# Two more column groups by seven products for eight: the third of the second eighth and the gate's first 512 columns

## The chip, the cores and the metric

The kernel runs on one core of a Trainium2 chip. TensorE (PE) multiplies; its weight loads (PEld) are shown apart. ScalarE (ACT) and VectorE (DVE) copy, round, add and apply functions, GpSimd (POOL) does a little arithmetic and issues some transfers, SyncE (SP) issues the weight transfers. The metric is the device time of one execution in microseconds; less is better. The time before is 2023.53 us, the median of 3 runs (2023.32 to 2023.73).

## The reference

Two layers over 256 positions of width 2048, batch 1, all in float32:

```python
h = rms_norm(x, norm1_g[l])
z = h @ w_in[l]
q, k, v, gu, gv = jnp.split(z, splits, axis=-1)        # 1024 columns each
attn = dilated_attention(rotary(q), rotary(k), v)      # 8 heads of 128
gm = chunked_gmlp(gelu(gu), gelu(gv), ln_g, ln_b, w_spatial, b_spatial)
x = x + concatenate([attn, gm]) @ w_out[l]
h2 = rms_norm(x, norm2_g[l])
x = x + square(relu(h2 @ w_up[l])) @ w_down[l]         # width 8192 between
```

and one last `rms_norm`. `chunked_gmlp` normalises its second argument (the columns `gv`, here "the gate") per group of 128, mixes it over positions with a masked 128x128 matrix per group, and multiplies by `gelu(gu)`.

## The kernel before

**Precision.** TensorE multiplies in a rounded form of float32 (`F32R`). Each factor is therefore split into a part hi, which ACT writes as a rounded copy, and a rest lo, which DVE writes as value minus hi. A product is the sum of three: hi by hi, hi by lo, lo by hi. So each block of weights of 128x1024 numbers (512 KB, one load of SP) costs ACT one copy (L168) and DVE one subtraction (L178) before TensorE can use it. The activations lie split in `hs` (the normalised input, L287 and L291), in `half` tiles (L646 and L649) and in `shared`.

**Three forms of product.** `transposed` (L376) keeps weights in the array and streams 256 positions: a step is 4 chunks of 128 rows by 256 columns, 24 matmuls of 256 columns. `natural` (L454) keeps activations in the array and streams 512 columns of weights: a step is 12 matmuls of 512. `fast` (L414) multiplies a block of 1024 rows by 512 columns as a 2 by 2 block matrix with seven products for eight (Winograd's form of Strassen's algorithm). It has two steps (p = 0, 1), called quick steps here, of 42 matmuls of 256 columns each: seven products of 2 chunks by 3 matmuls. Product by product, these use the weights' `top` block, `bottom` twice, `upper` twice and `lower` twice, where `upper` and `lower` are sums of blocks: four DVE additions (L219 to L224) on the raw weights. A quick step has two loads, but four blocks with a hi and a lo. It also needs sums of the left factor's blocks (four DVE additions, L803 to L806, then four times hi and lo). Its seven results lie in seven half banks of PSUM, and are added up later (`combine`, L815).

**Order.** The work is a list of steps written out by hand and traced once (L1007 to L1028). Every engine runs its instructions in the order in which this loop emits them. At step n it emits hi up to five loads ahead (`high_to`), what is due (`run_due`), lo up to four loads ahead (`low_to`), the loads of raw weights, then the step's matmuls, then what follows them (`after`, hooks), then at most 1.2 of cost from `queue` (`run_queue`). `later(delay, cost, fn)` and `soon(delay, fn)` count their delay in loads; a quick step counts as four (its four blocks). There are 6 hi and 6 lo buffers (L54 to L56), and 7 raw ones. A `mark` is a step without matmuls of its own; a `hook` runs behind the step with a given number.

**A layer.** `natural` over v (16 steps); `transposed` over k0, q0, k1, q1, k2, q2, k3, q3 (4 steps each, 32 in all, called q/k steps 0 to 31 here); `natural` over the gate (16 steps); `transposed` over gu (16) and over `w_out` (32). After each k or q follows its rotary (`after_qk`, L572: two ACT copies, three DVE operations); two loads after each q the scores of its two heads (`scores`, L587), before which the values of the previous two are multiplied (`values`); one load later the normalisation (`normalise`, L610), three loads later the transposes (`turn`). Behind each gate half come its gelu, statistics (`stats`, L672) and normalisation (`layer_norm`, L683, on POOL).

Then the MLP in eighths of 1024 hidden columns: stage e multiplies the e-th eighth of `w_up` (16 steps) and, one eighth behind, the rows of `w_down` of the eighth e - 1. Of the 2048 columns of `w_down`, the first 2 or 3 groups of 512 are done by quick steps, which are set before the steps that `ORDER` and `USUAL` (L63 to L66) name, one pair per group. The third group's partial results are added up in DRAM by POOL's transfers (`put`, L870). PSUM has 8 banks: 4 accumulators `acc`, of which the MLP's steps use two in turn, and 4 `aux`.

Of the kernel before, what the change touches and what calls it, by code (L numbers as in the profile page):

```python
# [61 lines left out]

ORDER = {1: ((7, 10), (13, 14)), 6: ((12, 15), (2, 3), (7, 8)), 7: ((7, 10), (2, 3)), 8: ()}  # L63
FINAL = (7, 7, 6)
# [3 lines left out]
HALVES = 5  # L68
BEHIND, BETWEEN = 2, 1
D_SCORES, D_NORM, D_TURN, D_VALUES = 2, 1, 3, 2  # L70

# [20 lines left out]
def trunk(ctx: ExitStack, tc: tile.TileContext, layout, xT, consts, gains, w, b_sp, w_sp, out):  # L92
# [8 lines left out]
    pacc = ctx.enter_context(tc.tile_pool(name="pacc", bufs=1, space=bass.MemoryType.PSUM))  # L101
    paux = ctx.enter_context(tc.tile_pool(name="paux", bufs=4, space=bass.MemoryType.PSUM))

# [31 lines left out]
    def acc_bank(i=None, of=4):  # L135
# [3 lines left out]
        return pacc.tile([P, 512], F32, name=f"acc{i}", tag=f"acc{i}")  # L139

    def aux_bank():
        return paux.tile([P, 512], F32, name="aux", tag="aux")

# [269 lines left out]

    def fast(name, l, row0, col0, tiles, slots, fresh, last, done):  # L414

# [5 lines left out]
        for p in range(2):  # L421
# [3 lines left out]
            def mm(p=p, top=top, bottom=bottom, upper=upper, lower=lower):  # L425
                if p == 0:
                    o.extend(slots())
                half = tiles[0][0]
                sums_ready()
                extra = sum_parts[0]  # L430
                left, right = slice(0, 256), slice(256, 512)
# [43 lines left out]
    def mark(fn):  # L475

        steps.append((None, fn, None))

    def from_hs(k):
# [38 lines left out]
    def layer(l, n1, n2, n3, last):  # L518
# [27 lines left out]
        if l:  # L546
            mark(start)
        mix_a, mix_g = [None], [None]
        qk = {}
# [37 lines left out]
        def scores(j, q, k):  # L587

            if turned:
                values(*turned.pop())  # L590
            s1, s0 = aux_bank(), aux_bank()
            for h in range(2):
                pe.matmul(s1[:, h * S:(h + 1) * S], lhsT=q[:, h, P:S], rhs=k[:, h, :], start=(h == 0), stop=True,  # L593
                          skip_group_check=True)
            for h in range(2):
                pe.matmul(s0[:, h * P:(h + 1) * P], lhsT=q[:, h, 0:P], rhs=k[:, h, 0:P], start=(h == 0), stop=True,  # L596
                          skip_group_check=True)
# [59 lines left out]
        def after_gv(c, ps):  # L657
            z, u = t32("gz", [2, 512], tag="tmpB"), t32("gu", [2, 512], tag="tmpA")
            for tt in range(2):
                act.activation(z[:, tt, :], ps[tt], AF.Copy, scale=n1.half[:, tt:tt + 1])  # L660

            def then(u, z):
# [4 lines left out]
                vec.scalar_tensor_tensor(par["y"][:, :, c:c + 512], u, 1.0, z, op0=OP.add, op1=OP.mult)  # L667
                later(1, 1.5, lambda: stats(c // P))

            gelu(z, u, then)  # L670

        def stats(g0):  # L672
# [8 lines left out]
            later(0, 1.0, lambda: layer_norm(g0))  # L681

        def layer_norm(g0):  # L683
            y, mv = par["y"], par["mv"]
            r = t32("lr", [2, 4])
            rsqrt(nc.gpsimd, r, mv[:, :, g0:g0 + 4, 1], 1.0, LN_EPS, [2, 4])
            for g in range(4):
                for tt in range(2):
                    yg = y[:, tt, (g0 + g) * P:(g0 + g + 1) * P]
                    nc.gpsimd.tensor_scalar(yg, yg, mv[:, tt, g0 + g, 0:1], r[:, tt, g:g + 1],  # L690
                                            op0=OP.subtract, op1=OP.mult)
            par["normed"] += 4
# [47 lines left out]
        hook(base + d + 6, rope)  # L740
        hook(base + d + 8, shift)
        for j in range(4):
            transposed("w_in", l, 0, KC, AW + j * 256, 256, from_hs, lambda c, ps, j=j: after_qk("k", j, ps))
            transposed("w_in", l, 0, KC, j * 256, 256, from_hs, lambda c, ps, j=j: after_qk("q", j, ps))
        natural("w_in", l, 4 * AW, AW, after_gv)
        transposed("w_in", l, 0, KC, 3 * AW, AW, from_hs, after_gu)
# [34 lines left out]
        def after_up(e):  # L781
            def f(c, ps):
# [17 lines left out]
        def sums():  # L800

            a11, a12, a21, a22 = (inner[:, 4 * k:4 * k + 4, t * P:(t + 1) * P] for t in range(2) for k in range(2))
            vec.tensor_tensor(a22, a21, a22, op=OP.add)  # L803
            vec.tensor_tensor(a21, a11, a21, op=OP.subtract)
            vec.tensor_tensor(a11, a22, a11, op=OP.subtract)
            vec.tensor_tensor(a12, a12, a11, op=OP.subtract)  # L806

# [4 lines left out]
            for k in range(0, 8, 2):  # L812
                later(0, 0.6, lambda k=k: parts(k))

# [33 lines left out]

        def halves(bank):
            return [bank[:, 0:256], bank[:, 256:512]]  # L850

        held = []
# [60 lines left out]
        for e in range(9):  # L913
# [3 lines left out]
            if e < 8:  # L917
                up = collect(transposed, "w_up", l, 0, KC, e * 1024, 1024, from_hs, after_up(e), of=2)
            if e:
                w = 512 * len(ORDER.get(e, USUAL))  # L920
                hidden = [hid[e - 1]]
                down = collect(transposed, "w_down", l, (e - 1) * 1024, 8, w, D - w, from_tiles(hidden, NH),
                               lambda c, ps, e=e, w=w: after_down(e, (c + w) // P, ps),
                               apart=last and e == 8, of=2 if e < 8 else 4,
                               cols=None if e < 8 else [c * P for c in LAST])
                for g, at in enumerate(ORDER.get(e, USUAL)):
                    banks = []
                    quick += zip(at, collect(fast, "w_down", l, (e - 1) * 1024, 512 * g, hidden,
                                             (lambda g=g, banks=banks: slots_other(g, banks)) if g else slots_first,
# [146 lines left out]
```

## Time and profile before

| | |
|---|---|
| median of 3 runs | 2023.53 us |
| the profiled execution, its time | 2023.7 us |
| its span in the profile | 2021.9 us |
| mean granted clock of TensorE | 0.997 |
| v, layer 0 | 7 to 51.6 us |
| q/k, layer 0 | 51.6 to 149.5 us |
| gate, layer 0 | 149.5 to 198.0 us |
| stage e = 1 (second eighth), layer 0 | 376.8 to 461.2 us |
| stage e = 3, layer 0 | 550 to 633 us |

The page gives each engine's busy time and share of the span, the chain of work that ended last, and groups of instructions with counts and mean durations. The trace behind it answers for windows of time, and lists instructions in order of time with the idle time before them and what ended it. Instructions of DVE and ACT overlap a little at their ends, so what counts in a sequence is the distance from start to start. A matmul's shown duration is longer than its slot, for the same reason.

### The profile page before, as it was taken

Reading aid. Unit: us, or ns where it says so; the run is one execution under the profiler, and the core shown is the slowest. Engines: PE = TensorE matmul, PEld = TensorE weight load, DVE = VectorE, ACT = ScalarE, POOL = GpSimd, SP = SyncE. Lnnn points to the kernel's source line nnn. Section 1 sums busy time; section 2 is a strip of 40 time slices with the busy share of each in tenths; the row PEclk is TensorE's granted clock in tenths of the full one; section 3 lists DMA queues with packets and bytes.
Section 4 is the critical chain, followed back from the end, with each engine's and each line's share of the span. In section 5 each row is a group of like instructions: output and inputs, shape, how many; then the busy total and the mean of one; then the engine's idle time right before and its main releaser. Section 6 shows DMA issues by size and latency. Waiting matters only on the chain.

```text
span 2021.9 us, 40716 instructions
## 1 busy us (share of the span) xinstructions
PE 2009.5 (99%) x16810; PEld 1973.4 (98%) x16810; DVE 1579.8 (78%) x1954; ACT 1221.2 (60%) x1613; POOL 156.2 (8%) x200
## 2 busy tenths in 40 slices
PE   9999999999999999999999999999999999999997
PEld 8998999999999999999989989999999999999997
DVE  7566766688888898898856667667888898888985
ACT  7565455566566666665645654556666666667653
POOL 0002300000001000100000032000000000010000
PEclk9999999999999999999999999999999999999998
DMA  9555556566678776866664555565676776777662
GB/s 330 192 167 167 187 189 202 174 229 204 222 219 239 240 225 203 249 215 215 201 215 158 168 187 188 188 199 179 217 229 208 228 236 216 239 220 241 212 215 81
DMA packets 126442, 419.26 MB, mean 207 GB/s; under 512 B 14128, under 2 KB 22064, under 8 KB 126256
## 3 DMA queue, kind: packets, MB, share of 16 engines
q1 hardware_dynamic: 110800, 389.86, 57.2%
q0 software_dynamic: 14304, 23.86, 6.5%
q8 instruction: 131, 2.15, 0.4%
q10 hardware_dynamic: 1152, 2.94, 0.4%
q14 instruction: 55, 0.45, 0.1%
HBM read 394.58 MB, written 22.02 MB: 206 GB/s over the span
## 4 chain that ended last, share of the span: by engine, by line
PE 99%; DVE 0%; ACT 0%; issue 0%; DVEq 0%
PE acc L410 70%; PE acc L440 10%; PE aux L440 8%; PE acc L470 3%; PE acc L472 3%; PE acc L471 3%; PE aux L699 0%; PE aux L635 0%; PE aux L593 0%; PE aux L622 0%; PE aux L994 0%; DVE x L1038 0%; PE aux L596 0%; PE aux L637 0%; PE acc L846 0%; PE aux L539 0%
## 5 line engine op out<-in xcount | busy, mean ns | idle before, releaser
L168 ACT ACTIVATE hi<-raw 128x1024 fp32r<-128x1024 f32 (+1 forms) x817 | 836.9, 1050 | 487.5 <-DVE raw L220 216.2
L178 DVE TENSOR_TENSOR lo<-raw,hi 128x1024 fp32r<-128x1024 f32 (+1 forms) x817 | 965.3, 1214 | 143.4 <-ACT hi L168 140.4
L410 PE MATMUL acc<-hs,hi 128*128 128x256 f32 x5632 | 985.9, 277 | 0.0
L410 PEld LDWEIGHTS acc<-hs,hi 128*128 128x128 f32 x5632 | 857.9, 188 | 0.4 <-issue 0.2
L410 PE MATMUL acc<-hs,lo 128*128 128x256 f32 x2816 | 778.0, 276 | 0.0
L410 PEld LDWEIGHTS acc<-hs,lo 128*128 128x128 f32 x2816 | 528.7, 188 | 0.4 <-issue 0.2
L410 PE MATMUL acc<-half,hi 128*128 128x256 f32 x2688 | 462.2, 276 | 0.0
L410 PEld LDWEIGHTS acc<-half,hi 128*128 128x128 f32 x2688 | 406.7, 188 | 0.0
L410 PE MATMUL acc<-half,lo 128*128 128x256 f32 x1344 | 371.0, 276 | 0.0
L410 PEld LDWEIGHTS acc<-half,lo 128*128 128x128 f32 x1344 | 252.3, 188 | 0.0
L873 POOL DMA_DIRECT2D far<-ar x92 | 74.2, 816 | 1164.4 <-ACT ar L876 563.9
L440 PE MATMUL acc<-hi,shared 128*128 128x256 f32 x768 | 138.4, 276 | 0.0
L440 PEld LDWEIGHTS acc<-hi,shared 128*128 128x128 f32 x768 | 119.2, 188 | 0.0
L440 PE MATMUL aux<-hi,half 128*128 128x256 f32 x528 | 110.6, 276 | 0.0
L440 PE MATMUL acc<-lo,shared 128*128 128x256 f32 x384 | 106.0, 276 | 0.0
L649 DVE TENSOR_TENSOR half<-ar,half 128x512 fp32r<-128x512 f32 x72 | 49.8, 691 | 68.6 <-ACT half L646 68.6
L470 PE MATMUL acc<-hi,hs 128*128 128x512 f32 x256 | 101.8, 398 | 0.0
L472 PE MATMUL acc<-hi,hs 128*128 128x512 f32 x256 | 100.6, 393 | 0.0
L471 PE MATMUL acc<-lo,hs 128*128 128x512 f32 x256 | 100.3, 392 | 0.0
L440 PEld LDWEIGHTS aux<-hi,half 128*128 128x128 f32 x528 | 87.2, 188 | 0.0
L440 PE MATMUL aux<-hi,shared 128*128 128x256 f32 x448 | 80.7, 276 | 0.0
L510 DVE TENSOR_TENSOR x<-x,acc 128x512 f32<-128x512 f32 (+1 forms) x49 | 33.1, 675 | 59.1 <-PE acc L410 57.3
(150 smaller groups left out, 1955.3 us busy)
## 6 DMA issues: line engine op xcount, KB each, us to landing
raw<-in_w SPq DMA_DIRECT2D x731, 512.0 KB, 4.7
far<-ar POOLq DMA_DIRECT2D x60, 256.0 KB, 8.3
far<-ar POOLq DMA_DIRECT2D x32, 128.0 KB, 4.3
ar<-far POOLq DMA_DIRECT2D x12, 256.0 KB, 9.7
raw<-in_w SPq DMA_DIRECT2D x10, 256.0 KB, 5.1
x<-in_xT SPq DMA_DIRECT2D x7, 256.0 KB, 5.9
out<-x SPq DMA_DIRECT2D x7, 256.0 KB, 3.1
shared<-in_b_sp ACTq DMA_DIRECT2D x2, 512.0 KB, 7.7
```

The lines of the kernel that those rows point to most:

```text
L168: act.activation(self.h[:, j * m:(j + 1) * m], self.raw[:, j * m:(j + 1) * m], AF.Copy)
L178: vec.tensor_tensor(lo[:, r], self.raw[:, r], self.h[:, r].bitcast(F32), op=OP.subtract)
L410: pe.matmul(o, lhsT=lhs, rhs=xs[:, rhs, :], start=(first and j == 0), stop=(last and j == 2), skip_group_check=True)
L440: calls.append(lambda k=k, j=j, lhs=lhs, rhs=rhs: pe.matmul(o[n], lhsT=lhs, rhs=rhs, start=(p == 0 and k == 0 and j == 0 and n in fresh), ...
L470: pe.matmul(ps, lhsT=xh, rhs=hi, start=(k0 + k == 0), stop=False)
L471: pe.matmul(ps, lhsT=xh, rhs=lo, start=False, stop=False)
L472: pe.matmul(ps, lhsT=xl, rhs=hi, start=False, stop=(k0 + k == KC - 1))
L510: vec.tensor_tensor(xj, xj, ps[j][:, 0:S] if alone else pair(ps)[:, j, :], op=OP.add)
L649: vec.tensor_tensor(t[:, c:c + 2, 1, :], src, t[:, c:c + 2, 0, :].bitcast(F32), op=OP.subtract)
L873: nc.gpsimd.dma_start(far[g][:, r], src, **({} if e == max(g, 1) else {"accum_op": OP.add}))
```

## The change

Three things. In the second eighth (e = 1) the third group of 512 columns of `w_down`, too, goes by seven products, and the quick steps there are placed anew: before steps 2 and 5, 9 and 10, 13 and 14. So that the first can come so early, the first eighth takes its columns in another order, and the sums of its left factor are formed in two halves, the first after columns 0 and 512.

In the gate, the first 512 columns (2048 rows) go by seven products: two blocks of 1024 rows, whose quick steps stand before q/k steps 3, 6 and 17, 25. Their left factor is x by the gain (eight ACT copies, `seven_sums`), summed in the same way and split (`seven_parts`); for the second 1024 rows this is emitted ahead of q/k steps 11 to 15. Seven half banks (two `acc`, two `aux`) hold the results from step 3 on; `gather` adds them up five loads after the last, and the gelu follows in the remaining gate steps. The q/k steps use two accumulators in turn; while the aux banks are held, the second scores go into the accumulator not in use. The `half` tiles of the attention's and gate's results are shared with the sums.

The normalisation of the first gate half moves from POOL to DVE (the second stays on POOL), and the second half's gelu starts one load later. The partial sums of the third group start at e = 1 rather than 2.

```diff
-ORDER = {1: ((7, 10), (13, 14)), 6: ((12, 15), (2, 3), (7, 8)), 7: ((7, 10), (2, 3)), 8: ()}
+ORDER = {1: ((2, 5), (9, 10), (13, 14)), 6: ((12, 15), (2, 3), (7, 8)), 7: ((7, 10), (2, 3)), 8: ()}
+SEVEN, AGAIN = ((3, 6), (17, 25)), 11
...
-            s1, s0 = aux_bank(), aux_bank()
+            s1, s0 = aux_bank(), acc_bank(1 - bank_at[0]) if aux_held else aux_bank()
...
+        def seven_sums(rows):
...
+            f = seven["plain"][rows]
+            for k in range(NH):
+                c = NH * rows + k
+                act.activation(f[:, k, :], x[:, c, :], AF.Copy, scale=g_all[:, n1.g, c:c + 1])
+            strassen_sums(f, 0, 4)
+
+        def seven_parts(rows, k):
+            to_half(seven["sums"], k, seven["plain"][rows][:, k:k + 2, :])
+
+        def seven_done(o):
+            soon(5, lambda: gather(o))
+
+        def gather(o):
+            z = t32("gz", [2, 512], tag="tmpB")
+            p1, p2, p3, p5, p7, p6, p4 = o
+            c11, c12, c21, c22 = (z[:, tt, h * S:(h + 1) * S] for tt in range(2) for h in range(2))
+            act.activation(c12, p1, AF.Copy)
+            vec.tensor_tensor(c11, c12, p2, op=OP.add)
+            vec.tensor_tensor(c12, c12, p6, op=OP.add)
...
+            for tt in range(2):
+                act.activation(z[:, tt, :], z[:, tt, :], AF.Copy, scale=n1.half[:, tt:tt + 1])
+            aux_held.clear()
+            seven["z"] = z
...
-            rsqrt(nc.gpsimd, r, mv[:, :, g0:g0 + 4, 1], 1.0, LN_EPS, [2, 4])
+            e = nc.gpsimd if g0 else vec
+            rsqrt(e, r, mv[:, :, g0:g0 + 4, 1], 1.0, LN_EPS, [2, 4])
...
+        hook(base + 13, lambda: seven_sums(0))
+        for k in range(0, NH, 2):
+            hook(base + 14 + k // 2, lambda k=k: seven_parts(0, k))
...
-        natural("w_in", l, 4 * AW, AW, after_gv)
+        quick = {}
+        for rows in range(2):
+            quick.update(zip(SEVEN[rows], collect(fast, "w_in", l, 1024 * rows, 4 * AW, seven_forms(rows), seven_slots,
+                                                  () if rows else (0, 2, 4, 6), range(7) if rows else (),
+                                                  seven_done if rows else None)))
+        if l:
+            mark(lambda: bank_at.__setitem__(0, 1))
+        for i, one in enumerate(plain):
+            if quick.get(i):
+                steps.append(quick[i])
+            if i == AGAIN:
+                mark(lambda: seven_sums(1))
+            if AGAIN < i <= AGAIN + 4:
+                mark(lambda k=2 * (i - AGAIN - 1): seven_parts(1, k))
+            steps.append(one)
+        late = collect(natural, "w_in", l, 4 * AW + 512, 512, lambda c, ps: soon(1, lambda: after_gv(512, ps)))
+        for i, one in enumerate(late):
+            if i == 6:
+                mark(lambda: gate_half(0, seven["z"]))
+            steps.append(one)
...
+                if e == 0 and c == 512:
+                    new_shared(F32R)
+                    sum_parts[0] = shared[0].rearrange("p (k h t) -> p k h t", k=NH, h=2)
+                    later(1, 1.0, lambda: sums([0]))
                 if c == 768:
                     summed[0] = False
-                    if e == 0:
-                        new_shared(F32R)
-                        sum_parts[0] = shared[0].rearrange("p (k h t) -> p k h t", k=NH, h=2)
-                    later(1, 1.5, sums)
+                    later(1, 1.5, lambda: sums([0, 1] if e else [1]))
...
-            nc.gpsimd.dma_start(far[g][:, r], src, **({} if e == max(g, 1) else {"accum_op": OP.add}))
+            nc.gpsimd.dma_start(far[g][:, r], src, **({} if e == 1 else {"accum_op": OP.add}))
...
-                up = collect(transposed, "w_up", l, 0, KC, e * 1024, 1024, from_hs, after_up(e), of=2)
+                up = collect(transposed, "w_up", l, 0, KC, e * 1024, 1024, from_hs, after_up(e), of=2,
+                             cols=None if e else (0, 512, 256, 768))
```

More of the change, by code (lines that the diff above doesn't have):

```diff
@@ L101, in trunk @@
     pacc = ctx.enter_context(tc.tile_pool(name="pacc", bufs=1, space=bass.MemoryType.PSUM))
-    paux = ctx.enter_context(tc.tile_pool(name="paux", bufs=4, space=bass.MemoryType.PSUM))
+    paux = ctx.enter_context(tc.tile_pool(name="paux", bufs=1, space=bass.MemoryType.PSUM))
     vec, act, pe = nc.vector, nc.scalar, nc.tensor
@@ L139, in acc_bank @@
         return pacc.tile([P, 512], F32, name=f"acc{i}", tag=f"acc{i}")
+    aux_at, aux_held = [3], set()
     def aux_bank():
-        return paux.tile([P, 512], F32, name="aux", tag="aux")
+        i = next(j % 4 for j in range(aux_at[0] + 1, aux_at[0] + 5) if j % 4 not in aux_held)
+        aux_at[0] = i
+        return paux.tile([P, 512], F32, name=f"aux{i}", tag=f"aux{i}")
     class Sub:
@@ L412, in transposed, with fast @@
             steps.append((wt, mm, (lambda c=c: after(c, accs[c])) if k0 + 4 == nk else None))
-    def fast(name, l, row0, col0, tiles, slots, fresh, last, done):
+    def fast(name, l, row0, col0, forms, slots, fresh, last, done):
         o = []
@@ L427, in mm @@
                     o.extend(slots())
-                half = tiles[0][0]
-                sums_ready()
-                extra = sum_parts[0]
+                half, extra = forms()
                 left, right = slice(0, 256), slice(256, 512)
@@ L477, in mark, with strassen_sums, halves @@
         steps.append((None, fn, None))
+    def strassen_sums(f, i, n):
+        a11, a12, a21, a22 = (f[:, 4 * k + i:4 * k + i + n, t * P:(t + 1) * P] for t in range(2) for k in range(2))
+        vec.tensor_tensor(a22, a21, a22, op=OP.add)
+        vec.tensor_tensor(a21, a11, a21, op=OP.subtract)
+        vec.tensor_tensor(a11, a22, a11, op=OP.subtract)
+        vec.tensor_tensor(a12, a12, a11, op=OP.subtract)
+    def halves(bank):
+        return [bank[:, 0:256], bank[:, 256:512]]
     def from_hs(k):
@@ L547, in layer @@
             mark(start)
+            mark(lambda: bank_at.__setitem__(0, 2))
         mix_a, mix_g = [None], [None]
@@ L667, in then, with seven_slots @@
                 vec.scalar_tensor_tensor(par["y"][:, :, c:c + 512], u, 1.0, z, op0=OP.add, op1=OP.mult)
-                later(1, 1.5, lambda: stats(c // P))
+                if c:
+                    later(1, 1.5, lambda: stats(c // P))
+                else:
+                    stats(0)
             gelu(z, u, then)
+        seven = {}
+        def seven_slots():
+            if "o" not in seven:
+                banks = [acc_bank(2), acc_bank(3)]
+                for _ in range(2):
+                    banks.append(aux_bank())
+                    seven.setdefault("aux", []).append(aux_at[0])
+                aux_held.update(seven["aux"])
+                seven["o"] = [h for b in banks for h in halves(b)][0:7]
+            return seven["o"]
@@ new lines, in seven_forms @@
+        def seven_forms(rows):
+            return lambda: (hs[:, NH * rows:NH * (rows + 1)], seven["sums"])
+        def seven_sums(rows):
+            if "sums" not in seven:
+                f = tp.tile([P, 2, NH, S], F32, name="plain", tag="half", bufs=2)
+                seven["plain"] = [f[:, i, :, :] for i in range(2)]
+                seven["sums"] = tp.tile([P, NH, 2, S], F32R, name="half", tag="half", bufs=2)
+            f = seven["plain"][rows]
[3 more added lines that the diff above has]
+            strassen_sums(f, 0, 4)
@@ L680, in stats @@
                     vec.bn_aggr(mv[:, tt, g0 + g, :], st[:, tt, g, :])
-            later(0, 1.0, lambda: layer_norm(g0))
+            if g0:
+                later(0, 1.0, lambda: layer_norm(g0))
+            else:
+                soon(1, lambda: layer_norm(0))
         def layer_norm(g0):
@@ L791, in f, with sums @@
                 to_half(hid[e][0], c // P, z, True)
+                if e == 0 and c == 512:
+                    new_shared(F32R)
+                    sum_parts[0] = shared[0].rearrange("p (k h t) -> p k h t", k=NH, h=2)
+                    later(1, 1.0, lambda: sums([0]))
                 if c == 768:
                     summed[0] = False
-                    if e == 0:
-                        new_shared(F32R)
-                        sum_parts[0] = shared[0].rearrange("p (k h t) -> p k h t", k=NH, h=2)
-                    later(1, 1.5, sums)
-            return f
[L800 to L806, printed above, removed]
+                    later(1, 1.5, lambda: sums([0, 1] if e else [1]))
+            return f
+        def sums(ps):
+            strassen_sums(inner, 2 * ps[0], 2 * len(ps))
             def parts(k):
@@ L812, in sums @@
             for k in range(0, 8, 2):
-                later(0, 0.6, lambda k=k: parts(k))
+                if k % 4 // 2 in ps:
+                    later(0, 0.6, lambda k=k: parts(k))
         def combine(place, c, banks, o=None):
@@ L847, in turn_back @@
             soon(1, lambda: update(n3, c, ps, False, last))
-        def halves(bank):
-            return [bank[:, 0:256], bank[:, 256:512]]
         held = []
@@ L927, in layer @@
                     banks = []
-                    quick += zip(at, collect(fast, "w_down", l, (e - 1) * 1024, 512 * g, hidden,
+                    quick += zip(at, collect(fast, "w_down", l, (e - 1) * 1024, 512 * g, forms,
                                              (lambda g=g, banks=banks: slots_other(g, banks)) if g else slots_first,
```

23 lines of the change are left out of this document (18 added, 5 removed).

## The prediction

> **What bounds the kernel now.** I read the page's busy times, then the chain that ended last, then that chain in order of time.
>
> ```profile
> span 2021.9 us, 40716 instructions
> ...
> PE 2009.5 (99%) x16810; PEld 1973.4 (98%) x16810; DVE 1579.8 (78%) x1954; ACT 1221.2 (60%) x1613; POOL 156.2 (8%) x200
> ...
> PE 99%; DVE 0%; ACT 0%; issue 0%; DVEq 0%
> ```
>
> TensorE is busy for all but 12.4 us, and the chain is 99% TensorE: it waits for nobody. A matmul less is time won, as long as the engines that prepare operands still hide behind TensorE. So there are two questions: how many matmul slots go, and where ScalarE (ACT) or VectorE (DVE) comes too late. Rates, from the chain in order of time (start, duration, group):
>
> ```profile
> 176.03 0.24 PE acc L470
> ...
> 198.03 13.62 PE acc L410 x120
> ...
> 395.81 4.54 PE aux L440 x40
> ```
>
> From 176.03 to 198.03 run the 8 steps of the gate's second 512 columns, 96 matmuls of 512 columns: 229 ns each. Both the transposed form (13.62/120) and the seven-product form (4.54/40) take 113.5 ns for 256 columns. So a transposed step of 24 matmuls takes 2.72 us, a quick step of 42 takes 4.77 us.
>
> **The change: matmuls.** Gate, per layer: 96 wide matmuls (22.0 us) become 2 x 84 narrow ones (19.07 us): -2.9 us. Second eighth, per layer: 96 narrow ones (10.90 us) become 84 (9.53 us): -1.36 us. Over two layers -5.8 and -2.7: **-8.5 us**, if nothing waits.
>
> [...]
>
> **The change: preparation.** What a quick step costs DVE, from the timeline of the first one in the second eighth, and the summing of the left factor:
>
> ```profile
> 379.49 0.69 DVE L803 TENSOR_TENSOR ar<-ar 128x512 f32<-128x512 f32 x1
> ...
> 382.27 1.22 DVE L178 TENSOR_TENSOR lo<-raw,hi 128x1024 fp32r<-128x1024 f32 x1
> 383.41 1.29 DVE L649 TENSOR_TENSOR shared<-ar,shared 128x512 fp32r<-128x512 f32 x2
> ...
> 386.95 0.68 DVE L191 TENSOR_TENSOR lo<-raw,hi 128x512 fp32r<-128x512 f32 x1
> 387.56 1.22 DVE L178 TENSOR_TENSOR lo<-raw,hi 128x1024 fp32r<-128x1024 f32 x1
> 388.69 0.69 DVE L219 TENSOR_TENSOR raw<-raw 128x512 f32<-128x512 f32 x1
> ...
> 391.47 0.69 DVE L649 TENSOR_TENSOR half<-ar,half 128x512 fp32r<-128x512 f32 x1
> 392.08 3.49 DVE L178 TENSOR_TENSOR lo<-raw,hi 128x1024 fp32r<-128x1024 f32 x3
> ```
>
> Start to start: top low 0.61, a full low 1.14, four weight sums 2.78, so 0.61 + 3 x 1.14 + 2.78 = 6.8 us against 4.77 us of TensorE. The left factor's sums are 2.78 and its four halves 4 x 0.61: 5.2 us per 1024 rows. Per layer the gate adds 4 x 6.8 - 8 x 1.14 for the steps replaced, 10.4 of sums, 7 operations of 0.42 in the combining and about 4 us of normalisation moved from POOL: some 36 us. Is there room?
>
> ```profile
> 51.60:198.00 146.40, 146.40 (x1055) 136.62 (x1054) 90.70 (x127) 81.94 (x131) 9.80 (x18) 1.00 0.55 179
> ...
> 550.00:633.00 83.00, 83.00 (x734) 83.00 (x733) 72.71 (x83) 54.72 (x70) 7.83 (x9) 1.00 0.73 227
> ```
>
> Window, its length, then PE, PEld, DVE (the fourth figure), ACT, POOL. DVE would go to 127 of 143.5 us in the q/k and gate stage, 88%, which the eighths (72.71 of 83) already run at without a gap. The mean fits. What decides is order: ACT and DVE work in program order, and the operands of step n are written about five steps ahead (six hi and six lo buffers). I therefore followed both queues through each quick step.
>
> **Where it collides: the third quick step of the gate, before q/k step 17.** Steps count from 0; 8-11 are k1, 12-15 q1. The first head pair's scores come after step 9. Here is what follows them now: TensorE from the chain, then ACT, then DVE from their timelines.
>
> ```profile
> 81.88 11.31 PE acc L410 x96
> ```
> ```profile
> 84.70 1.04 ACT L168 ACTIVATE hi<-raw 128x1024 fp32r<-128x1024 f32 x1
> 85.65 1.48 ACT L614 ACTIVATE ar<-ar,den 128x256 f32<-128x256 f32 x4
> 87.03 1.04 ACT L168 ACTIVATE hi<-raw 128x1024 fp32r<-128x1024 f32 x1
> ```
> ```profile
> 84.83 0.18 DVE L611 RECIPROCAL den<-den 128x4 f32<-128x4 f32 x1
> 85.77 1.22 DVE L178 TENSOR_TENSOR lo<-raw,hi 128x1024 fp32r<-128x1024 f32 x1 [0.77 <-ACT hi L168]
> 89.34 0.69 DVE L579 TENSOR_TENSOR ar<-acc,cosR 128x512 f32<-128x512 f32 x1 [2.35 <-ACT ar L578]
> ...
> 91.28 3.49 DVE L178 TENSOR_TENSOR lo<-raw,hi 128x1024 fp32r<-128x1024 f32 x3
> ```
> A rotary (three operations) takes 89.34 to 91.28, 1.94 us. Two scaled copies of the kind that the change adds follow each other 0.41 us apart:
> ```profile
> 1008.01 0.51 ACT L287 ACTIVATE hs<-x,cols 128x256 fp32r<-128x256 f32 x1 [2.11 <-DVE x L510]
> ...
> 1008.42 0.49 ACT L287 ACTIVATE hs<-x,cols 128x256 fp32r<-128x256 f32 x1
> ```
>
> Take 81.88, the start of step 10, as 0. The mark ahead of step 11 puts eight scaled copies on ACT right behind the normalisation (which ends at 5.15) and the four sums on DVE behind the reciprocal (which ends at 3.1), ahead of the low of step 15. The copies take 8 x 0.41 = 3.3 us, so the sums can't start before 8.5: **DVE stands idle for 5.4 us** with that low queued behind. Then it has, in this order: sums 2.78; low of 15; rotary of k1 1.94; low of 16; three halves; top low; bottom low; four weight sums 2.78; the fourth half; upper low; rotary of q1 1.94; lower low. That is 2 x 2.78 + 5 x 1.14 + 5 x 0.61 + 2 x 1.94 = 18.2 us, ending at 26.7, and about 27.5 with 0.8 us of waits for ACT on the way (its half copy behind the upper hi, and q1's swapped copy behind the lower hi). The upper low ends at about 23.9.
>
> TensorE reaches step 17's quick step at 7 x 2.72 plus 0.65 for the six transposes: 19.7. It needs the upper low after 18 of its matmuls (21.9) and the lower low after 30 (23.2). So it waits about 2.1 and again 2.2 us: **4.3 us a layer, +8.6 us**. Lower bound 3.4 (no waits for ACT at all), upper 5.5 (0.1 us more at each hand-over). Steps 15 and 16 get their lows at 12.5 and 16.1 for 14.4 and 17.1, so they don't wait.
>
> **The scores behind quick steps** 17 and 25. There the lookahead, counted in loads, reaches one step past the quick one, so the low of the step after next stands behind the scores' DVE work.
>
> ```profile
> 131.12 0.87 PE aux L593 x4
> ...
> 131.79 0.69 DVE L649 TENSOR_TENSOR half<-aux,half 128x512 fp32r<-128x512 f32 x1 [1.80 <-ACT half L646]
> ...
> 134.50 1.22 DVE L178 TENSOR_TENSOR lo<-raw,hi 128x1024 fp32r<-128x1024 f32 x1
> ```
>
> From the end of the values products (131.12) to the end of that low is 4.6 us. TensorE has the scores (1.31), one step with two deferred matmuls (2.95) and one matmul more: 4.37. About 0.25 us of wait, four times: **+1.0 us** (0 to 2).
>
> **What I cost at nothing, and its cover.** Carried forward in the same way, with the slack: quick steps 3 and 6 of layer 0, lower low in time by 1.1 and 0.7 us, layer 1 more (its rope and shift come earlier); step 25, 0.6 us; combining at step 26, next low 0.4 us ahead. In the second eighth the pairs before 9, 10 and 13, 14 lie a step closer than today's and three accumulator copies fall between: upper low of the last in time by 0.1 us. Its halved sums are ready before step 2. If all of these covers were short by half a microsecond, that would be +4 to +5. The normalisation of the second half on POOL starts some 7 us later against TensorE:
>
> ```profile
> 216.80 10.70 POOL L690 TENSOR_SCALAR shared<-shared,mv,lr 128x128 f32<-128x128 f32 x8
> ...
> 235.22 0.89 PE aux L699 x8
> ```
>
> It ended 7.7 us ahead of its reader, which needs only the first half of the eight: covered. Four more POOL stores per layer (0.82 us each on an engine 8% busy) and two weight loads per 4.77 rather than 5.5 us (DMA share 0.55) hide too; PSUM banks kept aside are replaced by an accumulator read two steps earlier.
>
> **Sum.** The profiled run took 2023.7 us (span 2021.9 and 1.8 around it): 2023.7 - 5.8 - 2.7 + 8.6 + 1.0 = 2024.8. It lies 0.2 over the median 2023.53, so I give **2024.6 us**: the matmuls saved are paid back as waits.
>
> **Rivals.**
> *The cover holds*: ACT or DVE gets through the first sums 4 us sooner than I work out, for example because the lows aren't due where I put them. Then 2023.5 - 8.5 + 0..1 = 2015 to 2017. For it: 88% mean load, as in the eighths. Against it: 18 us of work in order for 14.7 us. Chance 0.22, with the cases where half the wait goes.
> *The backlog lasts until step 25* (the slower side): from step 17 to 25 DVE has 7 lows, two rotaries, 3 us behind the scores and the 6.8 of preparation, 21.7 us, in 25.0 of TensorE (8 steps and 3.3 for values, scores and transposes). It recovers 3.3, and the margin at 25 is 0.6. If DVE leaves step 17 over 3.9 us behind its usual lead, step 25 and the combining wait as well, up to the same 4.3 a layer: 2024.6 + 8.6 = 2033, half of it 2029. Chance 0.14.
> *The clock drops in the wait*:
>
> ```profile
> 1.06 5.06 PE aux L994 x22
> ...
> 81.44 0.44 PE aux L596 x4
> ```
>
> The first 128-column matmuls take 230 ns, later ones 110: a half clock for the first 5 us. If each wait were followed by such a stretch, 2.5 us would be lost a layer: 2029.6. My two waits stay below 2.3 us with 1.4 us of matmuls between, and no row of before shows how long a gap must be. [...] Chance 0.04.
> *Nothing is saved or lost* (the seven products not used as the diff says): 2023.5; chance 0.02.
>
> **How the numbers follow.** My forecast, waits that eat the gain, spans 2020 to 2027.5 and has 0.58. Faster or slower counts from 0.2%, 4 us, about what a measurement of this kernel can tell from no change. Same takes 0.58 and 0.02, 0.60; faster 0.22; slower 0.14 and 0.04, 0.18. The range 2016 to 2029 leaves out the lower half of the first rival and the dearer half of the second, some 0.2 together.
>
> **What would show it.** Right: idle time of TensorE in front of L440 in the quick step behind q1, about 2 us twice, in both layers, released by DVE L178; an idle DVE of about 5 us in front of the first sum. Wrong: a gapless TensorE there (then 2015), or waits as long at step 25 or in the second eighth. L440 should gain 504 matmuls, L470 to L472 together lose 192 and L410 loses 192 more.

## The result and the profile after

The changed kernel takes 2076.11 us (median of 4 runs, 2071.14 to 2077.73) against 2023.5: the ratio is 1.0256, with a 95% interval of 1.0238 to 1.0274. It is 52.6 us slower. The forecast was 2024.6 and the range ended at 2029, so the prediction is wrong by far more than any wait in it. The profiled execution took 2077.73 us.

The page of the changed kernel, to be read against the lines of the kernel before:

```profile
span 2076.0 us, 41187 instructions
...
PE 2054.2 (99%) x16930; PEld 2022.5 (97%) x16930; DVE 1660.9 (80%) x2108; ACT 1263.7 (61%) x1695; POOL 136.5 (7%) x166
...
PE 94%; DVE 3%; ACT 2%; issue 1%; DMA 1%; ACTq 0%; DVEq 0%; SPq 0%
```

TensorE's matmuls went from 16810 to 16930: 504 more narrow ones in quick steps, 192 fewer wide and 192 fewer narrow ones, as announced. By the announced rates that is 8.5 us less work. But PE's busy time rose by 44.7 us, from 2009.5 to 2054.2, while its idle time rose from 12.4 to only 21.8. So most of the loss is no wait. **TensorE works longer on fewer columns.**

The chain in order of time says where. Its columns are start, duration, group. First after, then before; the groups with the same count are the same kind of work (line numbers differ by 5):

```profile
79.98 10.78 PE acc L415 x95
...
204.30 14.14 PE acc L415 x120
...
255.94 93.28 PE acc L415 x792
...
411.57 10.78 PE acc L415 x95
456.39 22.51 PE acc L415 x191
491.75 11.20 PE acc L415 x95
```
```profile
247.90 89.78 PE acc L410 x792
...
478.99 10.78 PE acc L410 x95
504.87 10.78 PE acc L410 x95
528.03 21.66 PE acc L410 x191
```

A run of 191 matmuls takes 22.51 us after and 21.66 before; 792 take 93.28 and 89.78; 95 take 11.20 in one place of the changed kernel and 10.78, as before, in another. So a matmul of 256 columns has **two slots** here (a slot is the distance from one matmul's start to the next), 113.3 and 117.8 ns. The clock is not it; the windows of the two groups of 191, after and then before (length, PE, PEld, DVE, ACT, POOL, then the granted clock, DMA share, GB/s):

```profile
456.39:478.89 22.50, 22.50 (x193) 22.50 (x193) 20.25 (x24) 15.32 (x21) 1.08 (x2) 1.00 0.70 252
```
```profile
528.03:549.69 21.66, 21.66 (x194) 21.66 (x193) 19.86 (x25) 14.36 (x19) 1.08 (x2) 1.00 0.63 239
```

The distances from one matmul's start to the next, read from the trace, show where each slot begins and ends. Layer 0 of the changed kernel (layer 1 is alike):

```
from (us)  to      slot    what stands at its start
 52        91      113.3   end of v, whose matmuls are wide
 91        204     both, changing at scores, transposes and values
 204       352     117.8   last head pair's values, directly ahead of gu
 352       442     113.3   spread of the second norm (L333)
 443       895     117.8   a wait of 0.65 us ahead of the quick step before step 13, e = 1
 896       ...     113.3   transposes (L943)
```

Counted in groups of twelve, some 10,600 of the changed kernel's 15,800 narrow matmuls have the long slot, some 230 of before's 15,600. 10,400 more at 4.45 ns are **46 us**: per layer 17 between 443 and 895 us, 5.4 behind the gate, 1 in the q/k stage.

The rest are waits of TensorE. Its list in the changed kernel (engine, line, releaser: us in total, times, longest):

```profile
PE acc L443 <- DVE lo L183: 3.6, 2, 1.8
PE aux L443 <- DVE lo L183: 2.8, 2, 1.5
...
PE acc L415 <- DVE lo L183: 1.0, 4, 0.3
PE acc L443 <- ACT ar L886: 1.0, 2, 0.5
```

The first two rows are the forecast waits at q/k step 17's quick step, the third those at steps 18 and 26, the fourth the one at e = 1. The rows give the time an engine stood still by the modelled ends; measured from start to start, less a slot, the four waits at step 17 are 1.98, 1.79, 1.97 and 1.58 us, the four behind the quick steps 0.4 each, the two at e = 1 0.65. Together 10.2 us.

Last, the clock. In this execution it was halved for 6.83 us in both layers, from 1.1 us behind the first wait at step 17 on (117.2 to 124.0 us in layer 0):

```profile
117.00:124.00 7.00, 5.51 (x24) 4.86 (x23) 3.61 (x5) 1.36 (x2) 0.00 (x0) 0.52 0.68 205
124.00:131.00 7.00, 6.75 (x54) 6.45 (x54) 5.00 (x7) 4.59 (x12) 0.00 (x0) 1.00 0.19 58
```

That loses at most 3.4 us a layer; part of it lies in the second wait, where nothing is lost. The run of 2071.14 had a mean clock of 0.998, which leaves no room for such a stretch; the others had 0.994 and 0.995. Sum without it: 2023.5 - 8.5 + 46 + 10.2 = 2071.2, measured 2071.14; with the 6.8 us that it can cost at most 2078.0, measured 2077.73.

### The profile page after: what moved, and what is told of

Same layout as the page of the kernel before. It is cut to its first block, busy times and chain, and to the rows that moved or that the text cites. A ratio compares the mean times of both kernels' runs of the same rounds, so it can differ in the third digit from the quotient of the medians.

```text
span 2076.0 us, 41187 instructions
## 1 busy us (share of the span) xinstructions
PE 2054.2 (99%) x16930; PEld 2022.5 (97%) x16930; DVE 1660.9 (80%) x2108; ACT 1263.7 (61%) x1695; POOL 136.5 (7%) x166
## 4 chain that ended last, share of the span: by engine, by line
PE 94%; DVE 3%; ACT 2%; issue 1%; DMA 1%; ACTq 0%; DVEq 0%; SPq 0%
PE acc L415 65%; PE acc L443 11%; PE aux L443 9%; PE acc L474 2%; PE acc L475 2%; PE acc L473 2%; DVE lo L183 1%; ACT hi L173 1%; PE aux L650 0%; PE aux L774 0%; ACT plain L717 0%; DMA raw<-in_w 0%; DVE half L664 0%; ACT ar L621 0%; DVE ar L617 0%
## 5 line engine op out<-in xcount | busy, mean ns | idle before, releaser
L183 DVE TENSOR_TENSOR lo<-raw,hi 128x1024 fp32r<-128x1024 f32 (+1 forms) x829 | 981.0, 1216 | 136.6 <-ACT hi L173 133.3
L415 PE MATMUL acc<-hs,hi 128*128 128x256 f32 x5632 | 1010.3, 280 | 0.0
L415 PEld LDWEIGHTS acc<-half,hi 128*128 128x128 f32 x2560 | 391.6, 189 | 0.0
L415 PE MATMUL acc<-half,lo 128*128 128x256 f32 x1280 | 357.8, 280 | 0.0
L443 PE MATMUL acc<-hi,shared 128*128 128x256 f32 x832 | 154.5, 279 | 0.0
L443 PE MATMUL aux<-hi,half 128*128 128x256 f32 x608 | 130.7, 282 | 0.0
L443 PEld LDWEIGHTS aux<-hi,half 128*128 128x128 f32 x608 | 102.1, 191 | 0.0
L443 PE MATMUL acc<-hi,half 128*128 128x256 f32 x480 | 94.3, 280 | 1.0 <-ACT ar L886 1.0
L443 PE MATMUL aux<-lo,half 128*128 128x256 f32 x304 | 85.9, 283 | 2.8 <-DVE lo L183 2.8
L443 PEld LDWEIGHTS acc<-hi,half 128*128 128x128 f32 x480 | 77.3, 188 | 1.4 <-ACT ar L886 1.4
```

The lines of the kernel that those rows point to most:

```text
L183: vec.tensor_tensor(lo[:, r], self.raw[:, r], self.h[:, r].bitcast(F32), op=OP.subtract)
L415: pe.matmul(o, lhsT=lhs, rhs=xs[:, rhs, :], start=(first and j == 0), stop=(last and j == 2), skip_group_check=True)
L443: calls.append(lambda k=k, j=j, lhs=lhs, rhs=rhs: pe.matmul(o[n], lhsT=lhs, rhs=rhs, start=(p == 0 and k == 0 and j == 0 and n in fresh), ...
```

## The experiments

All but best2 and best3 are one execution each, set against the kernel before on the same chip. 21 executions of before on one chip lie between 2022.85 and 2024.00 us.

### Which part of the change it is

**e1_only**: the kernel before, with the second eighth's part alone. **gate_only**: the changed kernel with the second eighth's places and stores as before (the first eighth's column order stays).

The first edit of e1_only, against before (its halved sums, column order and stores from e = 1 are as in the change), then that of gate_only, against after:

```diff
-ORDER = {1: ((7, 10), (13, 14)), 6: ((12, 15), (2, 3), (7, 8)), 7: ((7, 10), (2, 3)), 8: ()}
+ORDER = {1: ((2, 5), (9, 10), (13, 14)), 6: ((12, 15), (2, 3), (7, 8)), 7: ((7, 10), (2, 3)), 8: ()}
```
```diff
-ORDER = {1: ((2, 5), (9, 10), (13, 14)), 6: ((12, 15), (2, 3), (7, 8)), 7: ((7, 10), (2, 3)), 8: ()}
+ORDER = {1: ((7, 10), (13, 14)), 6: ((12, 15), (2, 3), (7, 8)), 7: ((7, 10), (2, 3)), 8: ()}
...
-            nc.gpsimd.dma_start(far[g][:, r], src, **({} if e == 1 else {"accum_op": OP.add}))
+            nc.gpsimd.dma_start(far[g][:, r], src, **({} if e == max(g, 1) else {"accum_op": OP.add}))
```

> The second eighth's part of the change alone, on the kernel before. Theory A (a wait of TensorE can leave all matmuls behind it in a longer slot, 117.8 ns for 113.3, until something else interrupts the stream): the wait of 0.76 us in front of the quick step before step 13 stays, and the some 3850 narrow matmuls per layer from there to the seventh eighth take 4.45 ns more each, 17.1 us a layer: 2023.5 - 2.7 + 1.5 + 34.3 = 2056.6. Theory B (the longer slot comes with the gate's part: its bank rotation and the banks held aside, or the other order of names in PSUM): no long slots here, 2021 to 2022.

> The changed kernel with the second eighth's two groups as before (the first eighth's column order and halved sums stay). Theory A: no wait in the second eighth, so the slot there is 113.3 ns from the first eighth on; 2076.1 - 34.3 - 1.5 + 2.7 = 2043.0, with the long slots from the gate's end to the second normalisation still there. Theory B: the long slots stay throughout, 2077 to 2079.

Measured: 2054.95 and 2040.98 us, against 2023.44 on that chip. The smaller part, which was to win 2.7 us, costs 31.5; the gate's part, which was to lose 3.8, costs 17.5. Both lie near theory A's values, 2056.6 and 2043.0, and far from theory B's. In e1_only the long slot begins at the same wait. Its chain there runs through ACT (L787 is L886 of the changed kernel), and the 36 matmuls behind take 4.51 us with the first hand-over, later ones 4.24, where before has 4.08:

```profile
431.27 0.50 ACT ar L787
...
431.81 4.51 PE acc L440 x36
```

### Whether the wait at e = 1 starts it

**pair_later**: the changed kernel with that pair one step later. The matmuls are the same.

```diff
-ORDER = {1: ((2, 5), (9, 10), (13, 14)), ...
+ORDER = {1: ((2, 5), (9, 10), (14, 15)), ...
```

> The changed kernel with one pair of quick steps of the second eighth before steps 14 and 15 instead of 13 and 14; nothing else. The wait in front of it was for ACT to read the accumulator of step 11, which then has one step more. Theory A: no wait and so no long slots up to the seventh eighth, 2076.1 - 34.3 - 1.5 = 2040.3. If the long slot had nothing to do with that wait: 2074 to 2076.

Measured: 2039.93 us. One step of distance removes the wait, and with it 36 us, though the wait is 0.65 us a layer. (In this run, in gate_only and in values_earlier the half clock shows in one layer only, so up to 3.4 us of each difference from the changed kernel is the clock.) The groups behind the pair, which took 117.8 ns a matmul in the changed kernel (22.51/191, 11.20/95), in the chain of pair_later:

```profile
456.30 18.93 PE acc L415 x167
...
487.62 10.78 PE acc L415 x95
```

Both are at 113.4 ns.

### Whether transposes end the long slot

**e1_turns**: e1_only with four transposes of a constant into a free accumulator at the start of stage e = 2, in both layers; nothing reads their result.

```diff
+        def turns():
+            ps = acc_bank(3)
+            for j in range(4):
+                pe.transpose(ps[:, j * P:(j + 1) * P], ones, ident)
...
+                if e == 2 and i == 0:
+                    mark(turns)
```

> The kernel before with the second eighth's part only, and in both layers four idle transposes into a free accumulator at the start of stage e = 2. Theory A (a wait flips the matmuls of 256 columns from 113.3 to 117.8 ns, the longer slot lasts until transposes come, and it is what this part costs): without the idle transposes the long slot lasted from 431 to about 890 us of layer 0 and as long in layer 1; with them it lasts from the wait at 431 us only to about 455 us, and the time is 2022 to 2024 + about 1.5 us for the transposes and the rest of the long slots, so 2022.5 to 2026. Theory B (the longer slot belongs to what the changed stages do, for example to a third group by seven products in the second eighth, its transfers or its places): the slot goes back to 117.8 ns with the next quick steps, and the time stays at 2053 to 2057.

Measured: 2025.47 us, against 2054.95 without them (before takes 2023.4 on both chips). Four transposes a layer, 0.44 us each time, compute nothing and save 29.5 us. First the chain of e1_only, then that of e1_turns; the same steps of stage e = 2 are at their ends:

```profile
444.92 22.50 PE acc L410 x191
467.42 4.24 PE acc L440 x36
...
480.26 11.19 PE acc L410 x95
```
```profile
444.92 16.86 PE acc L410 x143
461.77 0.44 PE acc L917 x4
462.21 5.46 PE acc L410 x48
467.67 4.08 PE acc L440 x36
...
480.05 10.78 PE acc L410 x95
```

Up to 461.77 both are at 117.9 ns a matmul (16.86/143); behind the four transposes (L917) it is 113.5 (10.78/95) in the one and still 117.8 in the other. Theory B falls: in e1_turns 36 matmuls of the seven products take 4.24 us ahead of the transposes (439.86) and 4.08 behind them (467.67), so the slot is not a property of the seven products.

### The second long stretch

**values_earlier**: the changed kernel with only the last head pair's values a load earlier.

```diff
-                later(D_VALUES, 1.0, lambda: values(*turned.pop()))
+                later(1, 1.0, lambda: values(*turned.pop()))
```

> The changed kernel with only the last head pair's values one load earlier, so that natural steps stand between them and the gu steps. Theory A (the long slot from the gate's end to 352 us, some 1220 matmuls a layer, begins at the values products that run directly ahead of gu): these slots go to 113.3 ns, 2 x 1220 x 4.45 ns = 10.9 us less, at most 1.5 us given back as waits of the values for their transposed factors: 2065 to 2067, and the long slot from 442 to 895 us stays. Theory B (the long slot there comes from something else, such as the gate's sums or the normalisation on VectorE): 2074 to 2078.

Measured: 2064.78 us, 11.3 below the changed kernel's median and 13.0 below its profiled execution. By the trace 2,800 fewer matmuls have the long slot, 12.5 us; the rest is one half clock less and new waits of 0.4 us a layer ahead of the values. Its chain has the short slot in gu and in all that follows up to the second eighth:

```profile
203.55 13.62 PE acc L415 x120
...
253.42 89.78 PE acc L415 x792
```

### What makes a wait flip the slot

Nine to thirteen idle additions on VectorE (the number is in the run's name) behind step 8 of layer 0's first eighth delay the lows and make TensorE wait once, far from the change. Their results, and in wait12t those of four transposes six steps later, are not used.

```diff
+        def dummies():
+            for _ in range(9):
+                vec.tensor_tensor(stage[:, 0:1024], con, con, op=OP.add)
+        if l == 0:
+            hook(base + 8, dummies)
```

> The kernel before, with nine idle additions of 1024 columns on VectorE (10.3 us) behind step 8 of layer 0's first eighth, results unused. They fit into the lookahead of five steps, so TensorE shouldn't wait. Both theories: 2023.4 to 2023.6, no long slots beyond those of before.

> The same with twelve additions (13.7 us), about 0.9 us more than the lookahead covers: one wait of TensorE of about 1 us in the whole kernel, all else as before. Theory A (a wait can leave the matmuls behind it in the 117.8 ns slot until another interruption): some 4700 matmuls from 363 us to the transposes near 868 us take 4.45 ns more, 2023.5 + 1 + 21 = 2045. Theory C (the slot of 117.8 ns comes with where operands or results lie, and the wait only goes with it): 2024.5.

> The same as the twelve additions, and six steps later four transposes of a 128x128 block into an accumulator that nobody uses there (0.45 us), results unused. Theory A, if transposes are what ends the long slot: 2023.5 + 1 + 1 + 0.5 = 2026. If transposes do nothing to it: as with the additions alone plus 0.5.

> The kernel before with ten idle additions on VectorE behind step 8 of layer 0's first eighth (one more than in the run with nine, whose wait of 1.5 us left the slots at 113.3 ns); the additions' results are not used. Each addition is 1.2 us, so the wait should be 2.7 us. Theory A (a wait flips the slot only where the granted clock falls with it, as in the run with twelve): no fall of the clock, slots stay 113.3 ns, 2026.5 to 2028. Theory B (every wait is a new throw, whatever its length): long slots until the transposes at about 890 us, 2044 to 2048.

> As the run with ten idle additions, with eleven: a wait of about 4.0 us. Theory A: if the clock falls, the slots are 117.8 ns behind it until about 890 us and the time is 2047 to 2050; if it doesn't, 2027.5 to 2029. Theory B: either slot, whatever the clock does.

> As the run with ten idle additions, with thirteen: a wait of about 6.5 us. Theory A: the clock falls, the slots are 117.8 ns behind it as in the run with twelve, 2049.5 to 2052. Theory B: the slot can as well be 113.3 ns behind it, 2031 to 2034.

The wait is its length beyond a slot, the slot that of the matmuls behind it once the clock is back, all from the trace:

```
         time (us)  before   wait   half clock  slot behind it
wait9    2025.88   2024.39   1.53   none        113.3
wait10   2028.31   2023.44   2.80   3.41 us     113.3
wait11   2029.47   2023.44   4.06   6.83 us     113.3
wait12   2049.12   2024.39   5.31   3.41 us     117.8, up to the transposes at 894 us
wait13   2051.68   2023.44   6.57   6.83 us     117.8, likewise
wait12t  2032.19   2024.39   5.31   6.83 us     113.3 from its transposes on (382.5 us)
```

wait9 was expected to cause no wait; it did, and left the slot alone. So a wait alone need not flip it. In wait12 TensorE's instructions and the places of their operands are those of before, and the long slot comes all the same: theory C falls. wait12 and wait13 give the long slot and cost 17 and 22 us more than wait12t and wait11. With ten and eleven additions the clock fell too and the slot stayed short: the fall of the clock doesn't decide either, and theory A of these runs falls. At this place the slot stayed short behind the waits of 1.53, 2.80 and 4.06 us and was long behind those of 5.31 and 6.57; at e = 1 0.65 us was enough, in both layers of every profile that had that wait. Length by itself doesn't decide. What does is **open**.

### Against the waits at step 17

**sums_earlier**: the changed kernel with the eight copies and the sums for the second 1024 rows three q/k steps earlier.

```diff
-SEVEN, AGAIN = ((3, 6), (17, 25)), 11
+SEVEN, AGAIN = ((3, 6), (17, 25)), 8
```

> The changed kernel with the sums for the second 1024 rows of the gate ahead of q/k steps 8 to 12 instead of 11 to 15. My prediction's account: the two waits of 2.1 and 1.9 us in front of the weights' sums behind q1 go in both layers (8 us), and with them the half clock that follows (6.8 us long, about 3 us lost each): 2076.1 - 8 - 6 = 2062. If the waits come from the weights' preparation alone: no change, 2076.

Measured: 2071.09 us, what the changed kernel takes without the half clock. A miss for both theories. One of the two waits went, but what was left at the lower block was 2.24 us in layer 0 and 2.95 in layer 1, and a new one of 0.78 us stood ahead of the scores: the marks are steps that run the queue too, so the scores moved up a step.

**best1** puts the copies behind steps 6 to 8, the sums behind 8 and the halves behind 9, 11, 12, 13, as work behind steps and not as marks. It also takes the pair at 14, 15 and the earlier values.

```diff
-ORDER = {1: ((2, 5), (9, 10), (13, 14)), ...
+ORDER = {1: ((2, 5), (9, 10), (14, 15)), ...
-                later(D_VALUES, 1.0, lambda: values(*turned.pop()))
+                later(1, 1.0, lambda: values(*turned.pop()))
...
-            if i == AGAIN:
-                mark(lambda: seven_sums(1))
-            if AGAIN < i <= AGAIN + 4:
-                mark(lambda k=2 * (i - AGAIN - 1): seven_parts(1, k))
-            steps.append(one)
+            steps.append(behind_step(one, extra.get(i)))
```

> The changed kernel with three repairs: the pair of the second eighth before steps 14 and 15; the left factor's copies for the second 1024 rows spread behind q/k steps 6 to 8, their sums behind step 8, their halves behind 9 to 13, without extra marks; and the last head pair's values one gate step earlier, so that a gate step stands between them and the gu columns. Theory A: no wait in the second eighth (-35.8), no or little wait behind q1 (-8 to -4) and no half clock (-6), short slots from the gate's end on (-10.8): 2016 to 2020. If long slots from the gate's end on stay: 2027 to 2031.

Measured: 2022.09 us, against 2024.39: 54 us better than the change, above the 2016 to 2020 of theory A, and in this one execution 2.3 us below the kernel before. Waits of 1.6 and 1.15 us were left at the lower of step 17's quick step. In **best2** the halves stand behind 9, 10, 10 and 11, where VectorE idles for 2.3 us ahead of k1's rotary, and the gate's gelu is no mark any more. **best3** is best2 with one more edit:

```diff
-SEVEN, AGAIN = ((3, 6), (17, 25)), 11
+SEVEN, AGAIN = ((3, 6), (18, 26)), 11
```

> The changed kernel with the second eighth's last pair before steps 14 and 15, the eight scaled copies of the second 1024 rows behind q/k steps 6 to 8, their sums behind 8, their halves behind 9, 10, 10 and 11 (ahead of k1's rotary, where VectorE stood idle for 2.3 us), the gate's gelu behind a step and not as a step of its own, and the last values one load earlier. Theory A (waits and long slots are all that the change loses): with halves behind 9, 11, 12, 13 this took 2022.1 against 2024.4; the wait of 1.6 and 1.2 us at the lower of step 17's quick step should fall below 0.5, and the waits of the values (0.5 a layer) go: 2018 to 2020.5 against a kernel before of 2023.5 to 2024.4. Theory B (the halves only push the wait to another place, and the waits behind the quick steps grow): 2021 to 2024.

> As the run with the halves behind 9 to 11, but with the second pair of the gate's quick steps before q/k steps 18 and 26, one step later, so that the scores stand ahead of a quick step and not behind it. Theory A (the 0.4 us waits at steps 18 and 26 come from the low that stands behind the scores' work when the lookahead reaches past the quick step): these four waits (1.7 us in all) go, and VectorE has one step more: 2016.5 to 2019.5. Theory B (the scores' work on VectorE now stands ahead of the quick step's own lower): a wait of 0.5 to 2 us moves into the quick steps: 2019 to 2024.

best2: 2025.28 us against 2023.41 (11 and 21 runs; ratio 1.0008, interval 0.9999 to 1.0017), no better than the one run of best1. It lies above both ranges, but what theory B says happened: the wait moved and grew. Its ACT, then that of best1, at the same point:

```profile
97.70 1.14 ACT L661 ACTIVATE half<-plain 128x512 fp32r<-128x512 f32 x2
99.82 1.50 ACT L629 ACTIVATE ar<-ar,den 128x256 f32<-128x256 f32 x4 [0.99 <-DVE den L626]
101.22 1.04 ACT L173 ACTIVATE hi<-raw 128x1024 fp32r<-128x1024 f32 x1
102.29 0.60 ACT L592 ACTIVATE ar<-acc 64x512 f32<-64x512 f32 x1
```
```profile
97.89 1.48 ACT L629 ACTIVATE ar<-ar,den 128x256 f32<-128x256 f32 x4
99.28 1.04 ACT L173 ACTIVATE hi<-raw 128x1024 fp32r<-128x1024 f32 x1
100.34 0.60 ACT L592 ACTIVATE ar<-acc 64x512 f32<-64x512 f32 x1
```

The halves fill VectorE's idle time, but VectorE then reaches the normalisation's reciprocal 2.5 us later, ACT waits for it, and the copies of k1's rotary (L592), on which that idle time ended, come 1.95 us later. The idle time moved along. The wait at the lower grew to 2.10 and 2.81 us.

best3: 2019.80 us against 2023.41 (11 and 21 runs; ratio 0.9983, interval 0.9974 to 0.9992). It is 3.6 us, 0.2%, below the kernel before: a small gain, but all its runs (2019.43 to 2020.78) lie below all of before's. As theory A had it, no wait stands at a quick step any more, nor behind one, though the time ends 0.3 us above that theory's range; what is left of TensorE's waits in the stage is one row:

```profile
PE aux L608 <- DVE ar L596: 1.0, 2, 0.5
```

It still has some 1,030 long slots, mostly from the second scores at 118 us to the end of the q/k stage, in both layers; the second transposes didn't end them. With the 800 long slots more than before has, and those two waits (1.3 us from start to start), 2023.5 - 8.5 + 800 x 4.45 ns + 1.3 is 2019.9.

## Where the prediction was right and where it failed

**The step that failed** is the rate: "Both the transposed form (13.62/120) and the seven-product form (4.54/40) take 113.5 ns for 256 columns." The forecast took that for all narrow matmuls and any order of the steps. The row to doubt it was among those quoted: 81.88 with 11.31 us for 96 is 117.8 ns. It was used for its start alone and never divided. Measured, 10,600 of 15,800 narrow matmuls took 117.8 ns. That made 46 of the 52.6 us. No rival had it: they were waits, the clock, or nothing saved.

**The saved matmuls** were right: the counts agree, and in best3 the 8.5 us are there less the 4.9 us of long slots and waits that stayed.

**The third quick step of the gate** was right in mechanism and size. VectorE's idle time ahead of the first sum was worked out as 5.4 us:

```profile
95.01 0.18 DVE L626 RECIPROCAL den<-den 128x4 f32<-128x4 f32 x1
100.54 0.69 DVE L485 TENSOR_TENSOR plain<-plain 128x512 f32<-128x512 f32 x1 [5.36 <-ACT plain L717]
```

The waits of 2.1 and 2.2 us a layer came as 1.98 and 1.79, 1.97 and 1.58: 7.3 us for 8.6. (18 matmuls behind 19.7 end at 21.7 and 30 at 23.1, not at 21.9 and 23.2; the slip decides nothing.)

**The scores behind quick steps** cost 0.4 us four times, for 0.25, inside the 0 to 2 us given.

**The covers costed at nothing**: quick steps 3, 6 and 25 and the combining were covered. The second eighth was not: "upper low of the last in time by 0.1 us" followed VectorE, and the wait came from ACT. The quick step before step 13 takes over the accumulator that step 11 filled, and ACT had not yet read it:

```profile
439.95 1.06 ACT L173 ACTIVATE hi<-raw 128x1024 fp32r<-128x1024 f32 x1 [2.97 <-DVE raw L225]
441.40 1.06 ACT L173 ACTIVATE hi<-raw 128x1024 fp32r<-128x1024 f32 x1 [0.39 <-DVE raw L229]
442.37 0.36 ACT L988 ACTIVATE ar<-aux 128x256 f32<-128x256 f32 x1
442.63 0.59 ACT L886 ACTIVATE ar<-acc 128x512 f32<-128x512 f32 x1
```

That read (L886) stands behind two hi that wait for VectorE's sums of weights. Their chain goes back to the end of the quick step before step 10, at 433.94, which stands one step behind its partner, where before had three. That this closeness makes the difference was not tested by itself. TensorE's last matmul before the wait starts at 442.51, the next at 443.27. The wait cost 1.3 us in both layers and brought on 34 us.

**The clock** was given 0.04, the author's estimate, and 5 us; in three of four runs it cost 5 to 6.6 us over the run without. The half clock in the first 5 us of before was read from the 230 and 110 ns alone: the profile's granted clock, 1.00 from 1 to 6 us, doesn't show it. The condition named was that each wait stays below 2.3 us with 1.4 us of matmuls between; that didn't protect it. The clock fell behind the first wait of 1.98 us, before the second began, and behind 2.80 us in wait10, but not in the profile of best2 behind 2.10 and 2.81 us, in that of sums_earlier behind 2.24 and 2.95, nor behind 1.53 us in wait9. So the rival's condition, the length of a wait, doesn't separate the profiles with a fall from those without. What does was not shown.

**The range** held waits of every kind that could be worked out, and nothing for the work itself. Of the rivals, the one on the slower side, a backlog up to step 25, did not occur: no wait stands at the quick step before step 25.

## What to carry to other kernels

Before trusting a rate, divide every group of the chain that has the same instruction, not two of them; here a few rows that were off by 4% had a second slot (117.8 ns for 113.3), and a change of order put two thirds of the narrow matmuls into it. Price an interruption of TensorE's stream not by its length alone: here 0.65 us cost 17 us a layer, and moving one pair of steps by one step, or four idle transposes, took most of it back. When an engine that works in order is given more to do, follow what stands behind it on that engine, above all the copy that sets a PSUM bank free, and what that copy's own predecessors wait for (here ACT's read L886, behind two hi: 0.65 us).

## What the runs showed that was not expected

- Two slots of a 256-column matmul with its own weight load, 113.3 and 117.8 ns, both at a granted clock of 1.00 and with the other engines about as busy (VectorE 20.25 of 22.50 us and 19.86 of 21.66). The long one lasted from 443 to 895 us in layer 0 of the changed kernel, the short one from 352 to 442. From 456 to 478 us of the changed kernel, in a long stretch, 62 of 186 weight loads take 191 to 193 ns and the others 187 to 189; from 355 to 440 us, in a short one, all 749 take 187 or 188: the two differ in the weight loads too, which the busy share doesn't show.
- The slot changed either way at an interruption: behind before's first scores (82 us) it is 117.8 ns, behind its transposes at 93 us 113.5; behind the transposes at 126 and 157 us of best3 it was still 117.8 (19.79/168, 14.13/120). Behind the last head pair's values it was long directly ahead of gu (14.14/120, the changed kernel) and short with a natural step between (13.62/120, values_earlier). Which way it goes was the same in both layers and in every profile for the wait at e = 1. In the q/k stage it was not: in pair_later the stretch from 128 to 150 us is long in layer 0 (11.31/96 at 136.21) and its like in layer 1 short (10.90/96 at 1146.16). What decides it was not found.
- The length of a wait did not decide whether the clock fell: it did behind 1.98 us (the changed kernel) and 2.80 us (wait10), and not behind 2.81 us (best2) and 2.95 us (sums_earlier). Inside the kernel the half clock lasted 3.41 us in wait10 and wait12 and 6.83 us in wait11, wait13, wait12t and twice in the changed kernel, whose records of full clock ahead of (from 4.58 us on), between and behind the two falls are 112.64, 1020.58 and 914.77 us long: 33, 299 and 268 times 3.413 us. What decides on a fall and on its length was not found.
